# Diagonal blocks of 16 in place of 32 in the triangular inverse of a recurrence

## The chip, the core and the metric

The kernel runs on one core of one Trainium2 chip. The metric is the device time of one execution in microseconds (us), as the median of several executions. The engines are called as in the profile: PE is TensorE (matmul), PEld its weight loads, DVE is VectorE, ACT is ScalarE, POOL is GpSimd, and SP is SyncE, whose queue issues all of this kernel's transfers (DMA). Each engine works through its own instructions in order and waits for the others by semaphores.

## The reference

A two-layer decoder trunk on 1024 positions of width 1024, in float32. Layer 1 mixes by a recurrence (RWKV-7) over 16 heads of 64, layer 2 is differential attention over 8 heads, and a final norm ends it. The change lies in layer 1:

```
def step(state, inp):
    r_t, w_t, k_t, v_t, a_t, b_t = inp
    sa = einsum('bhij,bhj->bhi', state, a_t)
    state = (state * w_t[:, :, None, :] + sa[..., None] * b_t[:, :, None, :]
             + v_t[..., None] * k_t[:, :, None, :])
    y_t = einsum('bhij,bhj->bhi', state, r_t)
    return state, y_t
```

with `a = -kk` and `b = kk * a_h`, where `kk` is normalised per head. Around it stand four projections of 1024x1024 (r, k, v and the gate g), two small low-rank products (`w`, `a`), a group norm of `y`, the gate and an output projection.

## The kernel before

The recurrence is done in chunks of 64 positions. Within a chunk the steps that depend on each other are put into a lower triangular 64x64 matrix per head, and its inverse, `q`, turns the chunk's values into updates with plain matmuls. A pass works on 8 chunk-heads at once for each half of the partitions: two chunks (NC) times four head pairs (NU). There are 16 such passes ("chunk pairs"), each with five parts, written as generators:

- `prep` loads the pass's operands, forms the products of keys and decays on DVE and ACT, and multiplies them on PE into `pm` (the triangular matrix and its companions). The diagonal blocks go by way of `ab` to a DRAM buffer `dA` and come back transposed in meaning as `al`: one diagonal block per partition.
- `invert` inverts every diagonal block. DVE scales `al` by the reciprocals `ni` of its last row and sets the diagonal of `xx`. Then POOL substitutes forward, step by step: a product into `tm` (line 551) and a sum into `xx` (line 553), 31 times for blocks of 32. The result is stored to DRAM as `dX` and loaded as `qd`, which has the blocks' rows on the partitions.
- `merge` puts the two blocks of 32 of each chunk-head together to `q` (64x64): DVE transposes `qd`, PE multiplies with the off-diagonal block of `pm` (line 586), DVE and ACT copy the product out of PSUM (590, 591), PE multiplies again (597), and DVE and ACT copy it into `q` (600, 601).
- `chain` is the recurrence over the two chunks with the state on PE (lines 639, 649, 658 and the outputs 629, 632).
- `norm` does the group norm of the outputs (683, 693 on PE) and stores to `d_o`.

The slots run from -3 to 16. In slot i the code emits `chain` of pass i, `norm` of i-1, `merge` of i+1, `prep` of i+3 and `invert` of i+2, each spread over 13 ticks (T), and between them a budget of other work per slot (FILL): the projections that have not been done yet (lines 192 to 194 on PE, `fl`) and later a part of the output projection (lines 285 to 287). A planner then sets the order of all instructions: it simulates the program with durations of its own (Durations) and puts first what is ready and has the higher priority (PRI; chain over merge over invert over prep over the rest). So the order on each engine follows from the emitted code, but isn't written out in it.

What the steps touch: tiles `al` and `xx` have two buffers each; the PSUM tile `mg`, one buffer, is used by `merge` (two times a pass) and by `norm` (two times). The SP queue issues all transfers in one order, and the loads `al` (waits for `dA`) and `qd` (waits for `dX`) stand in it among the loads for the projections.

Of the kernel before, what the change touches and what calls it, by code (L numbers as in the profile page):

```python
# [20 lines left out]
P = 128  # L21
# [11 lines left out]
T = 13  # L33
# [43 lines left out]
class Trunk:  # L77
# [317 lines left out]
    def wkv_open(self):  # L395
        nc, tc = self.nc, self.tc
# [9 lines left out]
        cst = st.enter_context(tc.tile_pool(name="wcst", bufs=1, reuse_waits="tile"))  # L406
# [7 lines left out]
        for r0 in (0, 64):  # L414
            v = self.pmask[r0:r0 + 64].rearrange("p a (z t) -> p a z t", z=2)
# [8 lines left out]
        self.last = cst.tile([P, P], F32, name="last")  # L424
        nc.gpsimd.memset(self.last, 0.0)
        for o in (0, 64):
            nc.gpsimd.memset(self.last[o:o + 64, o + 31:o + 64:32], 1.0)
        self.omka = cst.tile([P, KT], F32, name="omka")
        nc.vector.tensor_scalar(self.omka, self.par[:, COL["a_k_a"], :], -1.0, 1.0, op0=ALU.mult, op1=ALU.add)
        self.state = [cst.tile([P, NU, C], F32, name=f"st{j}") for j in range(KT // NU)]  # L430
# [12 lines left out]
    def prep(self, M, following):  # L443

        nc, tp, ua, ps = self.nc, self.tp, self.ua[M["n"] // 2 % 2], self.sps
        j = M["j"]
        cc, kk, a, r, v = (M[n] for n in ("cc", "kk", "a", "r", "v"))
        M["dA"] = dA = self.dr.tile([8, 4, 32, 32], F32, name="dA")

        def ch(x):  # L450
            return x.rearrange("p u (c t) -> p (u c) t", t=C)
# [31 lines left out]
        ab = tp.tile([P, 8, 32], F32, name="ab")  # L483
# [24 lines left out]
        for b in range(4):  # L508
            bs = slice(32 * b, 32 * b + 32)
            nc.vector.tensor_tensor(ab[bs], ab[bs], pm[bs, b // 2, :, b % 2 * 32:b % 2 * 32 + 32], op=ALU.add)  # L510
        nc.sync.dma_start(out=dA.rearrange("c x s t -> (x s) c t"), in_=ab)
        yield 0
        M["bkt"] = bkt = ua.tile([P, 2, 8, C], F32, name="bkt")
        for h in range(2):
# [9 lines left out]
        nc.vector.tensor_tensor(v.rearrange("p u t -> p (u t)"), pp, v.rearrange("p u t -> p (u t)"), op=ALU.mult)  # L524
        M["bv"] = self.dr.tile([P, NU, TM], F32, name="d_bv", bufs=6)
        nc.sync.dma_start(out=M["bv"], in_=v)
        M["al"] = al = self.sb.tile([P, 32, 32], F32, name="al", bufs=2)
        nc.sync.dma_start(out=al, in_=dA.rearrange("c x s t -> (c x) (s t)").unsqueeze(0).to_broadcast([4, 32, 1024]))
        if following:
            self.load(following)  # L530

    def invert(self, M):

        nc, sb, sm = self.nc, self.sb, self.sm
        al = M["al"]
        yield 1
        ni = sm.tile([P, 32], F32, name="ni")
        nc.vector.tensor_scalar(ni, al[:, 31, :], 1e-24, -1.0, op0=ALU.max, op1=ALU.mult)
        nc.vector.reciprocal(ni, ni)
        nc.vector.tensor_tensor(al[:, 0:31], al[:, 0:31], ni.unsqueeze(1).to_broadcast([P, 31, 32]), op=ALU.mult)  # L540
        xx = sb.tile([P, 8, 32], F32, name="xx")
        nc.gpsimd.memset(xx, 0.0)
        for k in range(4):
            xq = xx[k * 32:k * 32 + 32].rearrange("p c t -> p (c t)")[:, k::36]
            nc.vector.tensor_copy(out=xq, in_=ni[k * 32:k * 32 + 32, k::4])  # L545
        yield 0
        for s in range(31):
            n, w = s // 4 + 1, 31 - s
            tm = sb.tile([P, 128], F32, name="tm", bufs=1)
            tv = tm[:, 0:n * w].rearrange("p (c t) -> p c t", t=w)  # L550
            nc.gpsimd.tensor_tensor(tv, al[:, s:s + 1, s + 1:].to_broadcast([P, n, w]),  # L551
                                    xx[:, 0:n, s:s + 1].to_broadcast([P, n, w]), op=ALU.mult)
            nc.gpsimd.tensor_tensor(xx[:, 0:n, s + 1:], xx[:, 0:n, s + 1:], tv, op=ALU.add)  # L553
            yield 0
        dX = self.dr.tile([32, 8, 4, 32], F32, name="dX")
        nc.sync.dma_start(out=dX.rearrange("x k q t -> q x k t"), in_=xx)
        M["qd"] = qd = self.ub.tile([P, 8, 32], F32, name="qd", bufs=1)
        nc.sync.dma_start(out=qd, in_=dX.rearrange("(c x) k q t -> (x k q) c t", c=8))

    def merge(self, M):  # L560

        nc, ps = self.nc, self.wps
        pm, ar, qd = M["pm"], M["ar"], M["qd"]
        M["q"] = q = self.ub.tile([P, 8, C], F32, name="q")

        M["uv"] = uv = self.ub.tile([P, 2, 8, C], F32, name="uv")
# [2 lines left out]
        for h in range(2):  # L569
            for c in range(NC):  # L570
                t0 = M["qt"] * TM + c * C
                src = self.d_vc[t0:t0 + C, e0:e0 + NU * P].rearrange("p (u z e) -> p u z e", z=2, e=64)[:, :, h, :]
                nc.sync.dma_start(out=uv[64 - h * 64:P - h * 64, h, c::NC, :], in_=src)
        yield 1
        x1 = self.ub.tile([P, 8, 32], F32, name="x1", bufs=1)
        nc.vector.transpose(x1, qd)
        for o in (0, 64):
# [152 lines left out]
    def layer1(self):  # L730
# [51 lines left out]
        for i in range(-3, 17):  # L782
            st_ = []
            if i == 13:
                fl = itertools.chain(fl, self.run(self.out_proj(512, 2, I["a_w_out"][0])))
            if 0 <= i < 16:
                st_.append((self.chain(Ms[i]), 8, 0, T))
            if 0 <= i - 1 < 16:
                st_.append((self.norm(Ms[i - 1]), 6, 0, T))
            if 0 <= i + 1 < 16:  # L790
                st_.append((self.merge(Ms[i + 1]), 9, 2, T))
            if 0 <= i + 3 < 16:
                st_.append((self.prep(Ms[i + 3], Ms[i + 4] if i < 12 else None), 12, 0, T))
            if 0 <= i + 2 < 16:
                st_.append((self.invert(Ms[i + 2]), 34, 0, T))
            self.slot(T, st_, fl, FILL[i + 3])
        for _ in fl:
            pass
# [539 lines left out]
```

## Time and profile before

| | us |
|---|---|
| median of 3 runs | 1633.68 |
| lowest, highest | 1631.85, 1635.23 |
| the profiled execution | 1635.44 |
| its span | 1633.6 |
| PE busy | 1494.4 |
| DVE busy | 1194.8 |
| ACT busy | 909.6 |
| POOL busy | 672.8 |

The profile is of one execution. Its span begins with its first instruction and ends with its last; the device time is 1.8 us longer. The profile's busy time of PE runs over pipelined matmuls with modelled ends, and PE's clock is granted at one of two levels, 1.2 or 2.4 GHz; the profile gives the granted clock of a stretch as a share of the full one. The kernel begins with norm, low-rank products and projections (to about 270 us), goes through the stage of the recurrence with the rest of the projections between it (to about 910 us), and then does layer 2.

### The profile page before, as it was taken

Reading aid. Unit: us, or ns where it says so; the run is one execution under the profiler, and the core shown is the slowest. Engines: PE = TensorE matmul, PEld = TensorE weight load, DVE = VectorE, ACT = ScalarE, POOL = GpSimd, SP = SyncE. Lnnn points to the kernel's source line nnn. Section 1 sums busy time; section 2 is a strip of 40 time slices with the busy share of each in tenths; the row PEclk is TensorE's granted clock in tenths of the full one; section 3 lists DMA queues with packets and bytes.
Section 4 is the critical chain, followed back from the end, with each engine's and each line's share of the span. In section 5 each row is a group of like instructions: output and inputs, shape, how many; then the busy total and the mean of one; then the engine's idle time right before and its main releaser. Section 6 shows DMA issues by size and latency. Waiting matters only on the chain.

```text
span 1633.6 us, 31095 instructions
## 1 busy us (share of the span) xinstructions
PE 1494.4 (91%) x10496; PEld 1208.3 (74%) x10496; DVE 1194.8 (73%) x3119; ACT 909.6 (56%) x2095; POOL 672.8 (41%) x1685
## 2 busy tenths in 40 slices
PE   3799999988998999979869789999999999999897
PEld 3577777666776777768758567788888888888786
DVE  7745658866879798788555777887878888787764
ACT  5645565745657586655234644665565656556420
POOL 4000003856878688778656111233232333333100
PEclk8799999989999999979879789999999999999999
DMA  7654677755656567656446451211111111113231
GB/s 195 187 185 144 186 226 216 201 163 152 194 157 175 164 179 190 185 160 174 128 142 164 131 169 58 67 46 31 46 46 27 46 33 40 40 40 119 92 126 52
DMA packets 218095, 207.39 MB, mean 127 GB/s; under 512 B 78032, under 2 KB 163280, under 8 KB 217936
## 3 DMA queue, kind: packets, MB, share of 16 engines
q1 hardware_dynamic: 217936, 205.40, 42.9%
q8 instruction: 83, 1.36, 0.3%
q14 instruction: 76, 0.62, 0.1%
HBM read 147.09 MB, written 58.27 MB: 126 GB/s over the span
## 4 chain that ended last, share of the span: by engine, by line
PE 63%; DVE 14%; DMA 7%; ACT 6%; issue 5%; POOL 4%; SPq 1%; ACTq 0%; DVEq 0%; POOLq 0%
PE pj L878 6%; PE pj L877 6%; PE pj L879 6%; PE fl L192 5%; PE fl L193 5%; PE fl L194 5%; PE tr L982 4%; PE sc L940 2%; PE sc L941 2%; PE tr L970 2%; POOL xx L553 2%; POOL tm L551 2%; DMA al<-dA 1%; PE sc L498 1%; PE tr L1255 1%
## 5 line engine op out<-in xcount | busy, mean ns | idle before, releaser
L192 PE MATMUL fl<-xh,wh 128*128 128x512 f32 x512 | 212.2, 420 | 11.2 <-DVE ev L217 8.8
L877 PE MATMUL pj<-wh,xh 128*128 128x512 f32 x512 | 214.1, 418 | 0.0
L193 PE MATMUL fl<-xl,wh 128*128 128x512 f32 x512 | 209.2, 410 | 3.7 <-DVE xl L151 3.7
L553 POOL TENSOR_TENSOR xx<-xx,tm 128x60 f32<-128x60 f32 (+24 forms) x496 | 196.8, 397 | 36.4 <-DVE xx L545 0.4
L194 PE MATMUL fl<-xh,wl 128*128 128x512 f32 x512 | 209.3, 410 | 0.0
L551 POOL TENSOR_TENSOR tm<-al,xx 128x60 f32<-128x60 f32 (+24 forms) x496 | 190.2, 383 | 40.4 <-DVE xx L545 4.0
L878 PE MATMUL pj<-wh,xl 128*128 128x512 f32 x512 | 202.7, 396 | 2.6 <-DVE xl L1216 2.6
L879 PE MATMUL pj<-wl,xh 128*128 128x512 f32 x512 | 202.1, 396 | 0.0
L157 DVE TENSOR_TENSOR wl<-wf,wh 128x512 fp32r<-128x512 f32 x160 | 119.0, 748 | 80.4 <-ACT wh L156 79.5
L946 ACT ACTIVATE p<-sc,mx 128x256 f32<-128x256 f32 (+7 forms) x128 | 94.6, 741 | 142.1 <-DVE mx L945 123.1
L926 POOL CAST kh<-kh 64x128 fp32r<-64x128 f32 x128 | 45.2, 353 | 263.4 <-ACT kh L918 250.0
L156 ACT CAST wh<-wf 128x512 fp32r<-128x512 f32 x160 | 97.6, 617 | 94.1 <-PE fl L193 71.6
L192 PEld LDWEIGHTS fl<-xh,wh 128*128 128x128 f32 x512 | 98.4, 192 | 40.3 <-issue 12.4
L193 PEld LDWEIGHTS fl<-xl,wh 128*128 128x128 f32 x512 | 99.0, 193 | 29.2 <-DVE xl L151 5.2
L194 PEld LDWEIGHTS fl<-xh,wl 128*128 128x128 f32 x512 | 98.7, 193 | 24.0 <-issue 1.4
L879 PEld LDWEIGHTS pj<-wl,xh 128*128 128x128 f32 x512 | 96.8, 189 | 21.9
L878 PEld LDWEIGHTS pj<-wh,xl 128*128 128x128 f32 x512 | 97.5, 190 | 19.6 <-DVE xl L1216 4.3
L877 PEld LDWEIGHTS pj<-wh,xh 128*128 128x128 f32 x512 | 97.5, 190 | 15.4 <-ACT xh L1215 0.2
L944 DVE TENSOR_REDUCE mx<-sc 128x1 f32<-128x256 f32 (+7 forms) x128 | 95.4, 753 | 0.8
L982 PEld LDWEIGHTS tr<-v,p 128*128 128x128 f32 x576 | 74.9, 194 | 7.8 <-ACT p L972 3.2
L982 PE MATMUL tr<-v,p 128*128 128x128 f32 x576 | 76.1, 278 | 2.1 <-ACT p L972 2.1
L940 PE MATMUL sc<-kh,q 128*128 128x512 f32 (+2 forms) x192 | 70.9, 378 | 4.0 <-issue 2.1
(295 smaller groups left out, 3695.3 us busy)
## 6 DMA issues: line engine op xcount, KB each, us to landing
wf<-in_a_w_in SPq DMA_DIRECT2D x64, 512.0 KB
d_in<-ev SPq DMA_DIRECT2D x64, 256.0 KB
wf<-in_b_w SPq DMA_DIRECT2D x64, 256.0 KB
xk<-d_xn SPq DMA_DIRECT2D x40, 256.5 KB
al<-dA SPq DMA_DIRECT2D x16, 512.0 KB
wf<-in_a_w_out SPq DMA_DIRECT2D x16, 512.0 KB
p<-d_x SPq DMA_DIRECT2D x10, 512.0 KB
d_c<-cc SPq DMA_DIRECT2D x16, 260.0 KB
```

The lines of the kernel that those rows point to most:

```text
L156: self.nc.scalar.copy(out=wh, in_=wf)
L157: self.nc.vector.tensor_tensor(wl, wf, wh.bitcast(F32), op=ALU.subtract)
L192: nc.tensor.matmul(G["ps"], lhsT=wh[:, kk, :], rhs=xh, start=(k == 0), stop=False)
L193: nc.tensor.matmul(G["ps"], lhsT=wh[:, kk, :], rhs=xl, start=False, stop=False)
L194: nc.tensor.matmul(G["ps"], lhsT=wl[:, kk, :], rhs=xh, start=False, stop=(k == KT - 1))
L551: nc.gpsimd.tensor_tensor(tv, al[:, s:s + 1, s + 1:].to_broadcast([P, n, w]), xx[:, 0:n, s:s + 1].to_broadcast([P, n, w]), op=ALU.mult)
L553: nc.gpsimd.tensor_tensor(xx[:, 0:n, s + 1:], xx[:, 0:n, s + 1:], tv, op=ALU.add)
L877: nc.tensor.matmul(pf, lhsT=self.X[i][0][:, k], rhs=wh, start=(k == 0), stop=False)
L878: nc.tensor.matmul(pf, lhsT=self.X[i][1][:, k], rhs=wh, start=False, stop=False)
L879: nc.tensor.matmul(pf, lhsT=self.X[i][0][:, k], rhs=wl, start=False, stop=(k == KT - 1))
L940: nc.tensor.matmul(sc[:, b:e], lhsT=q[:, m], rhs=H["kh"][:, m, b:e], start=True, stop=False)
L982: nc.tensor.matmul(po, lhsT=at[:, b, :], rhs=H["v"][:, b, :], start=(b == 0), stop=(b == i))
```

## The change

The diagonal blocks that POOL substitutes are 16x16 instead of 32x32. There are twice as many of them, in half as many steps, and 15 instead of 31 pairs of instructions.

In `prep`, two DVE instructions pick for every row the 16 columns of its own block out of `ab` (with a mask `hm` of two columns that says to which half of a block of 32 a row belongs) into `a2`. `dA`, `dX`, `al` and `xx` have half or a quarter of the size, and other leading dimensions. The load after the substitution is called `qc` (two buffers).

In `merge`, a further level comes first: ACT spreads `qc` into `qd` with the mask (block diagonal, 16 and 16), DVE transposes it (`x0`), PE multiplies with the blocks of `pm` on 32x32 tiles (32 matmuls of 16 columns), DVE scales the product out of PSUM into `g0`, PE multiplies with `qd` (32 matmuls again), and DVE adds the result to `qd`. From there the code is as before. All of it uses the `mg` buffer. `merge` now has 13 steps from tick 1 on instead of 9 from tick 2 on, and `invert` 18 instead of 34.

```diff
-            nc.gpsimd.memset(self.last[o:o + 64, o + 31:o + 64:32], 1.0)
+            nc.gpsimd.memset(self.last[o:o + 64, o + 15:o + 64:16], 1.0)
+        self.hm = cst.tile([P, 2], F32, name="hm")
...
+        self.g0 = cst.tile([P, 8, 32], F32, name="g0")
+        nc.gpsimd.memset(self.g0, 0.0)
...
-        M["dA"] = dA = self.dr.tile([8, 4, 32, 32], F32, name="dA")
+        M["dA"] = dA = self.dr.tile([8, 4, 2, 16, 16], F32, name="dA")
...
-        nc.sync.dma_start(out=dA.rearrange("c x s t -> (x s) c t"), in_=ab)
+        a2 = tp.tile([P, 8, 16], F32, name="a2")
+        nc.vector.tensor_scalar(a2, ab[:, :, 0:16], self.hm[:, 0:1], None, op0=ALU.mult)
+        nc.vector.scalar_tensor_tensor(a2, ab[:, :, 16:32], self.hm[:, 1:2], a2, op0=ALU.mult, op1=ALU.add)
+        nc.sync.dma_start(out=dA.rearrange("c x b s t -> (x b s) c t"), in_=a2)
...
-        M["al"] = al = self.sb.tile([P, 32, 32], F32, name="al", bufs=2)
-        nc.sync.dma_start(out=al, in_=dA.rearrange("c x s t -> (c x) (s t)").unsqueeze(0).to_broadcast([4, 32, 1024]))
+        M["al"] = al = self.sb.tile([P, 16, 16], F32, name="al", bufs=2)
+        nc.sync.dma_start(out=al, in_=dA.rearrange("c x b s t -> (c x b) (s t)").unsqueeze(0).to_broadcast([2, 64, 256]))
...
-        for s in range(31):
-            n, w = s // 4 + 1, 31 - s
+        for s in range(15):
+            n, w = s // 2 + 1, 15 - s
...
-        dX = self.dr.tile([32, 8, 4, 32], F32, name="dX")
+        dX = self.dr.tile([64, 8, 2, 16], F32, name="dX")
         nc.sync.dma_start(out=dX.rearrange("x k q t -> q x k t"), in_=xx)
-        M["qd"] = qd = self.ub.tile([P, 8, 32], F32, name="qd", bufs=1)
-        nc.sync.dma_start(out=qd, in_=dX.rearrange("(c x) k q t -> (x k q) c t", c=8))
+        M["qc"] = qc = self.ub.tile([P, 8, 16], F32, name="qc", bufs=2)
+        nc.sync.dma_start(out=qc, in_=dX.rearrange("(c x) k q t -> (x k q) c t", c=8))
...
         yield 1
+        qd = self.ub.tile([P, 8, 32], F32, name="qd", bufs=1)
+        for b in range(2):
+            nc.scalar.activation(qd[:, :, b * 16:b * 16 + 16], qc, AF.Copy, scale=self.hm[:, b:b + 1])
+        x0 = self.ub.tile([P, 8, 32], F32, name="x1", bufs=1)
+        nc.vector.transpose(x0, qd)
+        yield 1
+        pg = ps.tile([P, 8, 32], F32, name="mg", bufs=1)
+        for c in range(8):
+            for x in range(4):
+                r = slice(32 * x, 32 * x + 32)
+                nc.tensor.matmul(pg[r, c, 0:16], lhsT=pm[r, x // 2, c, x % 2 * 32:x % 2 * 32 + 32], rhs=x0[r, c, 0:16],
+                                 start=True, stop=True, tile_position=(32 * x, 32 * x))
+        yield 1
+
+        nc.vector.tensor_scalar(self.g0[:, :, 0:16], pg[:, :, 0:16], self.hm[:, 1:2], None, op0=ALU.mult)
+        yield 1
+        pq = ps.tile([P, 8, 32], F32, name="mg", bufs=1)
+        for c in range(8):
+            for x in range(4):
+                r = slice(32 * x, 32 * x + 32)
+                nc.tensor.matmul(pq[r, c, 0:16], lhsT=self.g0[r, c, :], rhs=qd[r, c, 16:32], start=True, stop=True, tile_position=(32 * x, 32 * x))
+        yield 1
+        nc.vector.tensor_tensor(qd[:, :, 16:32], qd[:, :, 16:32], pq[:, :, 0:16], op=ALU.add)
...
-                st_.append((self.merge(Ms[i + 1]), 9, 2, T))
+                st_.append((self.merge(Ms[i + 1]), 13, 1, T))
...
-                st_.append((self.invert(Ms[i + 2]), 34, 0, T))
+                st_.append((self.invert(Ms[i + 2]), 18, 0, T))
```

Since the planner orders anew, the change moves instructions that it doesn't name. Two places show it.

On the SP queue late in the stage, about where the profile stands at 812 us, the order of before has the load `al` and, as the next transfer, the store `dX` of another pass (shapes are those of the destination):

```order
L511 DMA dA<-ab 128x8x32
L292 DMA d_x_68<-ev 128x256
L700 DMA d_o<-yt 128x4x128
L679 DMA bv<-d_bv 128x512
L528 DMA al<-dA 128x1x1024
L556 DMA dX<-xx 4x256x32
L526 DMA d_bv<-v 128x512
L292 DMA d_x_68<-ev 128x256
L278 DMA ev<-in_x 128x256
```

In the changed kernel, around a `dX` (line 567) of the same part of the stage, the `al` before it stands some 18 rows earlier, and the load `qc` (line 569) follows with one transfer between:

```order
L584 DMA uv<-d_vc 64x4x64 x4
L292 DMA d_x_68<-ev 128x256
L734 DMA d_o<-yt 128x4x128
L713 DMA bv<-d_bv 128x512
L567 DMA dX<-xx 2x512x16
L278 DMA ev<-in_x 128x256
L569 DMA qc<-dX 128x8x16
L239 DMA wf<-in_a_w_out 128x4x256
L522 DMA dA<-a_9289 128x8x16
```

What moved is the distance between `al` and `dX`: in the order of before they stand side by side four times, in the new one never, and the nearest are four transfers apart.

On PE in the middle of the stage, the order of before has one group of the merge (line 586) between the recurrence's matmuls and the projections (`fl`):

```order
L658 MATMUL zu<-uv,bkt 64x64
L632 MATMUL y<-pm,uv 64x64
L194 MATMUL fl<-xh,wl 128x512
L192 MATMUL fl<-xh,wh 128x512
L658 MATMUL zu<-uv,bkt 64x64 x7
L632 MATMUL y<-pm,uv 64x64 x7
L586 MATMUL mg<-x_4463,pm 32x32 x16
L193 MATMUL fl<-xl,wh 128x512
L194 MATMUL fl<-xh,wl 128x512
```

The changed kernel has there the second of the new groups (line 606; 673, 663 and 683 are the recurrence's lines 639, 629 and 649), behind 19 matmuls of the projections that stand after the first:

```order
L194 MATMUL fl<-xh,wl 128x512
L673 MATMUL zu<-sv,pm 64x64 x8
L663 MATMUL y<-ar,sv 64x64 x8
L606 MATMUL mg<-qd,g_1999 32x16 x13
L683 MATMUL zu<-zs,q 64x64 x8
L606 MATMUL mg<-qd,g_1999 32x16 x19
L192 MATMUL fl<-xh,wh 128x512
L193 MATMUL fl<-xl,wh 128x512
```

What moved: the short matmuls of merge and recurrence stand together in longer rows, and the projections' matmuls between them are spread over the same number of passes.

## Rows read from the trace of the kernel before

**Rows 1.** The page: PE's busy time, and POOL's busy tenths in 40 slices.

```profile
PE 1494.4 (91%) x10496; PEld 1208.3 (74%) x10496; DVE 1194.8 (73%) x3119; ACT 909.6 (56%) x2095; POOL 672.8 (41%) x1685
...
POOL 4000003856878688778656111233232333333100
```

**Rows 2.** Five stretches: length, busy PE, PEld, DVE, ACT, POOL, then clock, DMA, GB/s.

```profile
314.00:438.00 124.00, 110.44 (x952) 83.36 (x951) 87.52 (x173) 69.25 (x143) 84.67 (x202) 0.88 0.60 169
438.00:666.00 228.00, 214.71 (x2150) 164.63 (x2149) 182.53 (x417) 154.73 (x308) 179.71 (x417) 0.97 0.64 180
666.00:743.00 77.00, 65.03 (x784) 53.09 (x783) 64.86 (x153) 42.21 (x90) 59.01 (x137) 0.87 0.63 168
743.00:829.00 86.00, 72.20 (x886) 64.59 (x886) 54.22 (x138) 35.99 (x75) 52.46 (x139) 0.92 0.51 143
829.00:910.00 81.00, 64.42 (x849) 56.25 (x851) 53.62 (x208) 40.50 (x85) 46.54 (x129) 0.84 0.52 147
```

**Rows 3.** Groups by line, 314 to 910 us: busy us, mean ns | idle before, releaser.

```profile
L553 POOL TENSOR_TENSOR xx<-xx,tm 128x60 f32<-128x60 f32 (+24 forms) x462 | 181.1, 392 | 33.5
L551 POOL TENSOR_TENSOR tm<-al,xx 128x54 f32<-128x54 f32 (+24 forms) x461 | 174.4, 378 | 33.8
...
L540 DVE TENSOR_TENSOR al<-al,ni 128x992 f32<-128x992 f32 x14 | 19.0, 1354 | 0.4
...
L597 PE MATMUL mg<-qd,x 32*32 32x32 f32 x512 | 11.9, 197 | 5.2 <-DVE yt L696 5.2
...
L576 DVE STREAM_TRANSPOSE x<-qd 128x256 f32<-128x256 f32 x16 | 6.9, 431 | 0.3 <-DMA qd<-dX 0.3
...
L600 DVE COPY q<-mg 32x256 f32<-32x256 f32 x16 | 6.5, 405 | 0.4 <-PE mg L597 0.3
```

**Rows 4.** POOL in order of time: start us, length us, instruction.

```profile
854.25 0.23 POOL L551 TENSOR_TENSOR tm<-al,xx 128x28 f32<-128x28 f32 x1
854.57 0.24 POOL L553 TENSOR_TENSOR xx<-xx,tm 128x28 f32<-128x28 f32 x1
...
884.00 0.87 POOL L553 TENSOR_TENSOR xx<-xx,tm 128x28 f32<-128x28 f32 x1
...
886.43 0.21 POOL L553 TENSOR_TENSOR xx<-xx,tm 128x8 f32<-128x8 f32 x1
```

**Rows 5.** The chain of work, matmul groups (two records per matmul): start, us, what.

```profile
329.12 0.99 PE mg L586 x32
...
433.84 0.62 PE mg L597 x32
...
817.84 0.98 PE mg L683 x8
```

**Rows 6.** The SP queue in order of time: start us, length of the issue, transfer.

```profile
588.77 0.57 SPq L556 DMA_DIRECT2D dX<-xx  x1
589.44 2.18 SPq L168 DMA_DIRECT2D wf<-in_a_w_in  x1
...
593.60 0.37 SPq L558 DMA_DIRECT2D qd<-dX  x1
...
743.40 3.92 SPq L526 DMA_DIRECT2D d_bv<-v  x1
...
775.49 0.57 SPq L528 DMA_DIRECT2D al<-dA  x1
776.11 0.55 SPq L556 DMA_DIRECT2D dX<-xx  x1
776.75 9.74 SPq L239 DMA_DIRECT2D wf<-in_a_w_out  x1
```

**Rows 7.** PE in order of time, three waits: in brackets idle us and releaser.

```profile
368.10 0.76 PE L192 MATMUL fl<-xh,wh 128*128 128x512 f32 x1 [5.10 <-DVE ev L217]
...
792.62 0.58 PE L285 MATMUL fl<-wh,xh 128*128 128x256 f32 x1 [7.09 <-DVE ev L291]
...
831.68 0.44 PE L639 MATMUL zu<-sv,pm 128*64 128x64 f32 x2 [8.92 <-DVE sv L665]
```

More of the change, by code (lines that the diff above doesn't have):

```diff
@@ L426, in wkv_open @@
         for o in (0, 64):
-            nc.gpsimd.memset(self.last[o:o + 64, o + 31:o + 64:32], 1.0)
+            nc.gpsimd.memset(self.last[o:o + 64, o + 15:o + 64:16], 1.0)
+        self.hm = cst.tile([P, 2], F32, name="hm")
+        for b in range(2):
+            v = self.ident.rearrange("p (x b j) -> p b x j", b=2, j=16)[:, b]
+            nc.vector.tensor_reduce(self.hm[:, b:b + 1], v, axis=AX.XY, op=ALU.add)
+        self.g0 = cst.tile([P, 8, 32], F32, name="g0")
+        nc.gpsimd.memset(self.g0, 0.0)
         self.omka = cst.tile([P, KT], F32, name="omka")
@@ L536, in invert @@
         yield 1
-        ni = sm.tile([P, 32], F32, name="ni")
-        nc.vector.tensor_scalar(ni, al[:, 31, :], 1e-24, -1.0, op0=ALU.max, op1=ALU.mult)
+        ni = sm.tile([P, 16], F32, name="ni")
+        nc.vector.tensor_scalar(ni, al[:, 15, :], 1e-24, -1.0, op0=ALU.max, op1=ALU.mult)
         nc.vector.reciprocal(ni, ni)
-        nc.vector.tensor_tensor(al[:, 0:31], al[:, 0:31], ni.unsqueeze(1).to_broadcast([P, 31, 32]), op=ALU.mult)
-        xx = sb.tile([P, 8, 32], F32, name="xx")
+        nc.vector.tensor_tensor(al[:, 0:15], al[:, 0:15], ni.unsqueeze(1).to_broadcast([P, 15, 16]), op=ALU.mult)
+        xx = sb.tile([P, 8, 16], F32, name="xx")
         nc.gpsimd.memset(xx, 0.0)
-        for k in range(4):
-            xq = xx[k * 32:k * 32 + 32].rearrange("p c t -> p (c t)")[:, k::36]
-            nc.vector.tensor_copy(out=xq, in_=ni[k * 32:k * 32 + 32, k::4])
+        for k in range(2):
+            xq = xx[k * 64:k * 64 + 64].rearrange("p c t -> p (c t)")[:, k::18]
+            nc.vector.tensor_copy(out=xq, in_=ni[k * 64:k * 64 + 64, k::2])
         yield 0
-        for s in range(31):
-            n, w = s // 4 + 1, 31 - s
-            tm = sb.tile([P, 128], F32, name="tm", bufs=1)
+        for s in range(15):
+            n, w = s // 2 + 1, 15 - s
+            tm = sb.tile([P, 64], F32, name="tm", bufs=1)
             tv = tm[:, 0:n * w].rearrange("p (c t) -> p c t", t=w)
@@ L554, in invert @@
             yield 0
-        dX = self.dr.tile([32, 8, 4, 32], F32, name="dX")
+        dX = self.dr.tile([64, 8, 2, 16], F32, name="dX")
         nc.sync.dma_start(out=dX.rearrange("x k q t -> q x k t"), in_=xx)
-        M["qd"] = qd = self.ub.tile([P, 8, 32], F32, name="qd", bufs=1)
-        nc.sync.dma_start(out=qd, in_=dX.rearrange("(c x) k q t -> (x k q) c t", c=8))
+        M["qc"] = qc = self.ub.tile([P, 8, 16], F32, name="qc", bufs=2)
+        nc.sync.dma_start(out=qc, in_=dX.rearrange("(c x) k q t -> (x k q) c t", c=8))
     def merge(self, M):
         nc, ps = self.nc, self.wps
-        pm, ar, qd = M["pm"], M["ar"], M["qd"]
+        pm, ar, qc = M["pm"], M["ar"], M["qc"]
         M["q"] = q = self.ub.tile([P, 8, C], F32, name="q")
@@ L574, in merge @@
         yield 1
+        qd = self.ub.tile([P, 8, 32], F32, name="qd", bufs=1)
+        for b in range(2):
+            nc.scalar.activation(qd[:, :, b * 16:b * 16 + 16], qc, AF.Copy, scale=self.hm[:, b:b + 1])
[18 more added lines that the diff above has]
+        nc.vector.tensor_tensor(qd[:, :, 16:32], qd[:, :, 16:32], pq[:, :, 0:16], op=ALU.add)
         x1 = self.ub.tile([P, 8, 32], F32, name="x1", bufs=1)
```

## Prediction, made before the changed kernel ran

> **What bounds the kernel now.** I read the page first: TensorE (PE) is busy for 91% of the span, GpSimd (POOL) for 41%, but POOL's work lies in slices 7 to 23 alone, where it is busy for six to eight tenths [rows 1]. This is the stage of the recurrence, about 300 to 910 us, and only there does the change do anything. Next I cut that stage into five stretches [rows 2]. The reader is to see two things in them. First, PE and POOL are both nearly full: in the quiet middle (438 to 666 us) PE is busy 214.7 of 228 us, and POOL 179.7 us; POOL pauses some 0.08 us after each of its 417 instructions (854.25 + 0.23 to 854.57, [rows 4]), another 33 us, so it is held for 213 of 228 us. Second, the other stretches lose more of PE: idle time plus the part taken by the clock (one minus the granted clock, times the length) is 13.3 + 6.8 us in the middle, 9%, but 13.6 + 14.9 of 124 us (23%) ahead of it, 12.0 + 10.0 of 77 (29%) and 13.8 + 6.9 of 86 (24%) behind it, and 16.6 + 13.0 of 81 (37%) in the last stretch. Together that is 121 us. So PE is the engine that ends the stage, its work is fixed, and the question is how much of those 121 us comes back against the work that is added to PE.
>
> Where the losses come from is read from the waits. Three of PE's longest end with VectorE (DVE) work, 5.10, 7.09 and 8.92 us [rows 7], but DVE was itself held: just ahead of each, the SP queue issued the load `al` and, as its next transfer, the store `dX`, and then took 9.74 us over an issue that otherwise takes a fraction of one; a `dX` that does not follow an `al` costs the next issue 2.18 us [rows 6]. The order of before has four such pairs (at 349, 389, 775 and 817 us; one stands in the rows), and all three waits follow one.
>
> **POOL and the DVE work around the substitution.** Before, a chunk pair has 31 steps of two instructions, 62, at a mean of 392 and 378 ns [rows 3]: 62 x 0.385 + 62 x 0.08 = 28.8 us. Now it has 15 steps, 30 instructions, of at most 36 elements per partition. Small ones take 0.23 us undisturbed and 0.87 us disturbed [rows 4]; I take 0.35, so 30 x 0.43 = 13 us. POOL gets some 16 us per slot back, 250 us in all. Taken by itself this buys little: none of PE's long waits [rows 7] ends with POOL. It matters through the tail and through POOL's full load, below. On DVE the product over `al` shrinks from 992 to 240 elements: 1.35 us [rows 3] becomes about 0.35. Four copies into `xx` become two. Against that stand two small instructions ahead of the store `dA`, one more transpose (0.43 us, the row of L576), a scaling and an addition that read PSUM (0.2 to 0.41 us each, the upper end from L600, [rows 3]): 1.4 us removed, 1.2 to 1.7 us added. I put DVE at zero; ScalarE gets two small instructions and is busy for two thirds of the middle stretch [rows 2], which hides them.
>
> **PE: the price.** Each merge gets two groups of 32 matmuls on 32x32 tiles, with 16 moving columns. The trace has groups of 16 of the same weight shape with 32 columns: 0.62 us at the full clock, 0.99 us at the lower [rows 5]. From below: half the columns at half the price, so a group of 32 costs 0.62 us. From above: the same price per matmul at the lower clock, 1.98 us. Which end is nearer is told by L683, where 2 moving columns still cost 0.98 us for eight records [rows 5]: narrow matmuls are paid by the weight load, not by columns. So I take the full-clock price per matmul, 1.24 us, 2.48 us per slot, 16 slots: **+39.7 us** (20 to 63). Nothing hides it, since PE is the engine that ends the stage.
>
> **PE: what comes back.** (a) In the new SP order no `dX` follows an `al` directly (4 transfers lie between at the least, 10 or more after the first slots), and `al` moves 128 KB instead of 512. The three waits are 21.1 us. The clock ahead of and behind the middle lies under its 0.97: 124 x 0.09 + 86 x 0.05 = 15.5 us [rows 2]. I take the waits and 10 of the clock, **-31 us** (0 to -37). (b) In the last stretch the two last substitutions share POOL, the later one ends at 886.6 us [rows 4], and the merge and the recurrence of that pair can only follow it. PE's loss there above the middle's rate of 9% is 29.6 - 7.3 = 22 us. With two substitutions shorter by 16 us each I take a little more than half, **-13 us** (0 to -22). (c) With POOL at half its load, the middle stretch, where POOL was held for 93%, loses less: its 20.1 us cannot all go; I take **-9 us** (0 to -14). (d) Against these: the tile `mg` has one PSUM buffer, which served two merge groups and two norm groups per slot and now serves six. PE waits 5.2 us in all for the norm's reader ahead of L597 [rows 3]; half as much again is **+3 us** (0 to 10).
>
> Behind the added steps of the merge PE has other work standing (mostly 5 to 20 matmuls of the projections, as the order shows), so the two extra trips to DVE and ScalarE cost nothing as long as that work is there; in the last slots, where it runs thin, they cost part of what (b) gives, which is why (b) is not taken whole. The wait on `dX` that holds SP ahead of the load of `qc`, and what stands behind it, is in the rivals.
>
> Sum: 39.7 - 31 - 13 - 9 + 3 = -10 us on the profiled run's 1635.4 us. That run lies 1.8 us above the median, so against the median 1633.7 - 10 = 1623 or 1624; I say **1624 us**.
>
> **A rule beside the rows.** What the trace shows: `dX`, 128 KB, has landed 4.83 us after its issue when the load `qd` that waits for it goes out [rows 6], with a leading dimension of 4 at its destination; the change makes that 2, with pieces of half the size and the same number of them. The Trainium skill, page "DMA: Bandwidth & Descriptors", section "Rules for kernel authors", says that an outermost dimension of few entries, such as a leading broadcast, confines a DMA to as many engines at most. By it `dX` and `al` would go from four engines to two; `dX` would have twice the pieces on each, while `al`, with a quarter of the bytes, would still have half on each. No row of before tells two engines from four. In the sum it changes nothing; it is behind the third rival.
>
> **Rivals.** 1. Slower: *the added matmuls are paid and the losses only change place*. In-order DVE and SP are re-planned, and other transfers meet instead; short matmuls in a row let the clock fall again. For it: the stretch 666 to 743 us lost 29% with no such pair in it [rows 2]. Price: +39.7 + 3 with a third of (a) to (c), -18: +25, so 1659. It decides where less than some 40 us of the 121 come back. 2. No change: the price of a group is as taken and 40 of the 53 come back: 1634. For it: the terms cancel nearly by themselves. 3. Slower: *the way back of the inverse*. If `dX` takes twice its 4.83 us, the load `qc` behind it holds SP 4.8 us longer in each of 16 slots, 77 us; half of it on the path is +39, so 1663. Against it: the inverse itself is done some 16 us earlier, and an SP issue of 3.92 us at 743 us [rows 6] has no PE wait of note behind it. It decides if PE's waits follow `dX`, slot by slot. 4. Faster by more: a group costs 0.62 us, as columns say: 20 us less, 1604. That the change doesn't do what it says is no case here: the order shows 480 POOL instructions in place of 992.
>
> **How the numbers follow.** The forecast, 1624, gets 0.37 and rival 4 0.16, so faster by over 0.2% (about 3.3 us, what a measurement of this kernel can tell from no change) is 0.53. Rival 2 gets 0.12. Rival 1 gets 0.27 and rival 3 0.08: slower 0.35. The range reaches from 14 us below rival 4, where nearly all of (a) to (c) comes back as well, to rival 1 and a little past it: 1590 to 1663. The forecast's own range, if it is faster, is 1600 to 1630.
>
> **What will show it.** The two new groups in the trace: 1.24 us each (1.1 to 1.4) or nearer 0.62. POOL's two substitution lines: 480 instructions, about 170 us busy, not 387. The SP queue: no issue of 8 us or more behind `al` and `dX`. The granted clock between 314 and 438 us: near 0.97. The stage's last stretch: PE's loss under 25%. The time from `dX` to `qc`: 4.8 us or nearer 9.7. I am wrong if PE's idle time plus clock loss in the stage stays at 110 us or more, or if the groups cost 2 us each.

## The result: 1.1 % slower, and what the profile after shows

| | before | changed |
|---|---|---|
| median, us (4 runs each) | 1634.45 | 1653.66 |
| lowest, highest | 1631.85, 1639.30 | 1649.16, 1658.58 |
| ratio, 95% interval | | 1.0107 [1.0075, 1.0138] |
| profiled execution, its span | 1635.44, 1633.6 | 1658.58, 1656.9 |

The forecast was 1624, faster. It came out slower by 19 us, inside the range (1590 to 1663), near the first rival's 1659 and the third's 1663. The profiled run of the changed kernel is the slowest of its four, so the two spans below differ by 23 us.

The page of the changed kernel, against [rows 1]: GpSimd is relieved as planned, 434.8 us in place of 672.8, and TensorE is busier by 34 us.

```profile
PE 1528.1 (92%) x12544; PEld 1238.1 (75%) x12544; DVE 1185.4 (72%) x3169; ACT 922.0 (56%) x2127; POOL 434.8 (26%) x1174
...
POOL 4010013443323324233320011233333333333100
...
L562 POOL TENSOR_TENSOR tm<-al,xx 128x30 f32<-128x30 f32 (+10 forms) x240 | 74.5, 310 | 59.7 <-DVE xx L556 39.4
...
L564 POOL TENSOR_TENSOR xx<-xx,tm 128x30 f32<-128x30 f32 (+10 forms) x240 | 73.2, 305 | 18.1
```

To see where the stage lost its time, both kernels have to be cut at the same places of the program, since equal times are not equal work. The cuts here are the issues on the SP queue of the 1st, 7th, 11th and 16th store `d_o`, one per pass. The end is the start of what follows the stage, 648.5 us before the end of the span in both. Columns as in [rows 2]: length, busy PE, PEld, DVE, ACT, POOL, clock, DMA, GB/s. First the kernel before, cut that way:

```profile
280.00:436.41 156.41, 142.85 (x1112) 107.72 (x1111) 113.65 (x219) 92.10 (x187) 113.87 (x259) 0.90 0.60 171
436.41:658.25 221.84, 208.55 (x2084) 159.66 (x2083) 178.60 (x409) 148.74 (x297) 174.97 (x405) 0.97 0.65 181
658.25:813.98 155.73, 136.19 (x1647) 116.23 (x1645) 119.17 (x283) 80.98 (x170) 115.08 (x282) 0.90 0.58 159
813.98:953.46 139.48, 111.77 (x1194) 95.19 (x1191) 88.72 (x317) 65.78 (x140) 54.94 (x158) 0.83 0.50 146
953.46:985.10 31.64, 26.93 (x115) 20.80 (x114) 24.89 (x79) 15.99 (x43) 3.94 (x12) 0.89 0.58 182
280.00:985.10 705.10, 626.29 (x6141) 499.60 (x6140) 525.02 (x1304) 403.59 (x837) 462.79 (x1114) 0.91 0.59 167
```

And the changed kernel:

```profile
280.00:424.53 144.53, 133.97 (x1411) 101.26 (x1410) 103.01 (x214) 85.54 (x180) 62.53 (x158) 0.89 0.54 148
424.53:676.77 252.24, 241.07 (x3001) 185.72 (x3001) 186.34 (x446) 163.85 (x327) 83.57 (x221) 0.97 0.57 162
676.77:825.64 148.87, 129.15 (x1939) 109.45 (x1940) 103.31 (x274) 77.40 (x165) 49.75 (x141) 0.81 0.48 130
825.64:951.41 125.77, 109.27 (x1641) 96.00 (x1635) 84.26 (x291) 61.77 (x133) 18.72 (x50) 0.84 0.54 157
951.41:1008.40 56.99, 47.90 (x199) 38.11 (x199) 36.91 (x126) 25.51 (x65) 10.64 (x32) 0.85 0.41 128
280.00:1008.40 728.40, 661.37 (x8177) 530.54 (x8177) 513.83 (x1348) 414.07 (x867) 225.22 (x601) 0.89 0.53 149
```

Read the last row of each: TensorE idles 78.8 us before and 67.0 after, but the clock takes 63.5 us (0.09 of 705) before and 80.1 (0.11 of 728) after. The losses together are 142 and 147 us. So the whole loss did not shrink but grew by 5 us, and the added work came on top: busy time less the clock's part is 562.8 us before and 581.2 after, 18 us more. The worst stretch is the third, where the clock falls from 0.90 to 0.81. The fourth, the thinning end of the recurrence, is better as forecast: 51 us of loss became 37. But the fifth, behind the last store, lost 17.6 us where it had lost 8.2, so over the two of them 5 us are left. (It also had more to do, 47.9 us busy for 26.9: work moves between the stretches even with these cuts.)

How one of the waits there comes about can be read from three queues of the changed kernel. SP first:

```profile
714.50 0.53 SPq L567 DMA_DIRECT2D dX<-xx  x1
715.14 5.16 SPq L256 DMA_DIRECT2D xm<-d_o  x2
720.39 0.38 SPq L522 DMA_DIRECT2D dA<-a  x1
722.05 0.37 SPq L569 DMA_DIRECT2D qc<-dX  x1
```

then DVE, with idle time and releaser in brackets:

```profile
718.20 0.69 DVE L488 TENSOR_TENSOR bk<-kraw,a 64x512 f32<-64x512 f32 x1
722.74 0.69 DVE L259 TENSOR_TENSOR xm<-xm,xk 128x512 f32<-128x512 f32 x1 [3.85 <-DMA xm<-d_o]
723.47 0.41 DVE L634 COPY q<-mg 32x256 f32<-32x256 f32 x1
```

and PE:

```profile
717.68 2.08 PE L533 MATMUL sc<-sq,bones 128*128 128x512 f32 x2
724.03 0.45 PE L683 MATMUL zu<-zs,q 64*64 64x64 f32 x2 [4.27 <-DVE q L634]
```

The store `dX` is issued at 714.50; the two loads `xm` behind it hold the queue for 5.16 us; DVE, which works in order, stands 3.85 us before the product that needs `xm`; the copy of `q` is behind that product, and TensorE stands 4.27 us for `q`. It is the same pattern as `al` and `dX` in [rows 6] and the waits of [rows 7], without an `al` next to it. In the whole stage the issues right behind `dX` took 55.9 us in the 16 slots of before (their own length of some 0.4 us each included), of which 35.4 behind the four pairs, and 67.9 us in the changed kernel, with no pair at all: none longer than 5.41 us, but a long one in nearly every slot. From `dX` to `qc` it is now 7.5 to 9.9 us, where `qd` came 4.8 to 6.1 us behind a `dX` that stood alone (11.3 to 12.4 in the pairs).

A third thing hangs on `dX`: GpSimd. Its memset of the next `xx` (line 542 before, 553 after) waits for the store to be done with that tile. Over the stage (waited for: us, times, longest), before:

```profile
POOL xx L542 <- DMA dX<-xx: 47.9, 10, 13.0
```

and in the changed kernel:

```profile
POOL xx L553 <- DMA dX<-xx: 93.4, 14, 9.4
```

So part of the time that GpSimd got back went into a longer wait for the store.

The added groups on PE, at the full clock:

```profile
309.39 0.72 PE L596 MATMUL mg<-x,pm 32*32 32x16 f32 x64
310.05 0.50 PE L192 MATMUL fl<-xh,wh 128*128 128x512 f32 x1
```

310.05 - 309.39 = 0.66 us for 64 records, 10 ns each, where the 32 records of L597 with 32 columns took 0.62 us [rows 5], 19 ns each. Half the columns cost half; the two groups of 16 passes come to 2 x 0.66 x 16 = 21 us, not 39.7. (Their busy time in the stage is 12.9 and 16.3 us, since some ran at the lower clock.)

### The profile page after: what moved, and what is told of

Same layout as the page of the kernel before. It is cut to its first block, busy times and chain, and to the rows that moved or that the text cites. A ratio compares the mean times of both kernels' runs of the same rounds, so it can differ in the third digit from the quotient of the medians.

```text
span 1656.9 us, 34761 instructions
## 1 busy us (share of the span) xinstructions
PE 1528.1 (92%) x12544; PEld 1238.1 (75%) x12544; DVE 1185.4 (72%) x3169; ACT 922.0 (56%) x2127; POOL 434.8 (26%) x1174
## 4 chain that ended last, share of the span: by engine, by line
PE 64%; DVE 12%; DMA 10%; ACT 6%; issue 4%; POOL 2%; SPq 1%; DVEq 0%; ACTq 0%; POOLq 0%
PE pj L911 6%; PE pj L912 6%; PE pj L913 6%; PE fl L192 5%; PE fl L193 5%; PE fl L194 5%; PE tr L1016 4%; PE sc L974 2%; PE sc L975 2%; PE tr L1004 2%; DMA xm<-d_o 2%; PE sc L505 1%; DMA dX<-xx 1%; PE zu L673 1%; PE tr L1288 1%
## 5 line engine op out<-in xcount | busy, mean ns | idle before, releaser
L157 DVE TENSOR_TENSOR wl<-wf,wh 128x512 fp32r<-128x512 f32 x160 | 115.1, 724 | 77.6 <-ACT wh L156 74.6
L156 ACT CAST wh<-wf 128x512 fp32r<-128x512 f32 x160 | 97.2, 616 | 92.5 <-PE fl L193 83.7
L978 DVE TENSOR_REDUCE mx<-sc 128x1 f32<-128x256 f32 (+7 forms) x128 | 95.7, 754 | 0.8
L562 POOL TENSOR_TENSOR tm<-al,xx 128x30 f32<-128x30 f32 (+10 forms) x240 | 74.5, 310 | 59.7 <-DVE xx L556 39.4
L1016 PEld LDWEIGHTS tr<-v,p 128*128 128x128 f32 x576 | 74.5, 193 | 11.3 <-ACT p L1006 6.7
L564 POOL TENSOR_TENSOR xx<-xx,tm 128x30 f32<-128x30 f32 (+10 forms) x240 | 73.2, 305 | 18.1
```

The lines of the kernel that those rows point to most:

```text
L156: self.nc.scalar.copy(out=wh, in_=wf)
L157: self.nc.vector.tensor_tensor(wl, wf, wh.bitcast(F32), op=ALU.subtract)
L978: nc.vector.tensor_reduce(c, sc[:, 0:n], axis=AX.X, op=ALU.max)
L1016: nc.tensor.matmul(po, lhsT=at[:, b, :], rhs=H["v"][:, b, :], start=(b == 0), stop=(b == i))
```

## Experiments

Ratios are to the kernel before, run on the same chip. "Loss" is TensorE's idle time and what the clock took, worked out as above from the row from 280 us to 648.5 us before the end of the span (taken as the same in all versions); it is of one profiled run each, and the clock's part is an upper bound, as not all work scales with the clock.

**Relief, short matmuls, transfers.** Four kernels. The kernel before with every second step of the substitution left out (its inverse is incomplete), so GpSimd's relief without anything else:

```diff
-        for s in range(31):
+        for s in range(0, 31, 2):
...
-                st_.append((self.invert(Ms[i + 2]), 34, 0, T))
+                st_.append((self.invert(Ms[i + 2]), 18, 0, T))
```

> The kernel before, with every second step of the substitution left out (16 of 31 steps, 512 POOL instructions instead of 992, spread over 18 ticks' steps as in the changed kernel); blocks of 32, transfers and merge as before. The inverse is not computed rightly, the work is otherwise the same. It measures POOL's relief alone. Theory L (PE's work sets the stage; its losses only change place): within 6 us of before, 1628 to 1640. Theory W (the relief is real, but the slower way back of the inverse, dX on a leading dimension of 2, takes it): 1610 to 1620.

1640.57 us, 0.9988 [0.9963, 1.0014]. The relief alone is worth nothing here, although GpSimd's time in the span falls to 484.8 us: the loss is 142 us as before, and GpSimd's wait for `dX` is 64.5 us in place of 47.9.

The changed kernel with each new group of 32 short matmuls replaced by one wide one (the values are not those wanted):

```diff
-        for c in range(8):
-            for x in range(4):
...
+        nc.tensor.matmul(pg[:, :, 0:16], lhsT=pm[:, 0, 0, :], rhs=x0[:, :, 0:16], start=True, stop=True)
```

> The changed kernel with each of the two new groups of 32 short matmuls replaced by one matmul of 128 rows and 128 columns into the same PSUM tile (wrong values, same waits, same DVE and ScalarE steps). It takes 16 x (1.32 - 0.54) = 12.5 us of PE work away, the two groups having taken 0.66 us each and a single matmul of that size some 0.27. Theory L: 12 us faster than the changed kernel, about 1641. Theory W: no more than 5 us faster, 1648 to 1654. A third view, that rows of short matmuls lower the granted clock, gives more than 12 us: 1635 or less, with the clock of the stage back at 0.91.

1627.83 us, 0.9923 [0.9902, 0.9944]: by the ratios 1.8 %, 30 us, below the changed kernel, for 13 to 17 us of work left out (a group takes 0.66 us, the wide matmul 0.14 to 0.25). How much of that is the work and how much a new order can only be told with several orders of each kernel, below.

The changed kernel with `al` as two loads and `dX` as two stores of 64 partitions, so that no transfer has a leading dimension of 2:

```diff
-        nc.sync.dma_start(out=al, in_=dA.rearrange("c x b s t -> (c x b) (s t)").unsqueeze(0).to_broadcast([2, 64, 256]))
+        for k in range(2):
+            nc.sync.dma_start(out=al[k * 64:k * 64 + 64], in_=dA.rearrange("c x b s t -> (c x b) s t"))
...
-        nc.sync.dma_start(out=dX.rearrange("x k q t -> q x k t"), in_=xx)
+        for k in range(2):
+            nc.sync.dma_start(out=dX[:, :, k, :], in_=xx[k * 64:k * 64 + 64])
```

> The changed kernel with the store dX written as two stores of 64 partitions and the load al as two loads of 64 partitions, so that no leading dimension is 2; same bytes, same pieces, two more transfers per slot. By the Trainium skill's rule on leading dimensions dX should land in well under the 7.6 us from its issue to the load qc (3 to 4 us), and SP should not be held for 4 to 5 us behind it. Theory W: 12 to 20 us faster than the changed kernel, 1634 to 1642. Theory L: the waits go, but PE's time does not, within 6 us of it, 1648 to 1658.

1593.95 us, 0.9716 [0.9685, 0.9746]: by the ratios 3.9 %, 64 us, below the changed kernel and faster than before by 2.8 %. Far more than either theory had. The SP queue of this kernel at about the same time (one pass further on), and the stage as a whole:

```profile
712.50 1.22 SPq L569 DMA_DIRECT2D dX<-xx  x2
713.80 0.57 SPq L292 DMA_DIRECT2D d_x<-ev  x1
714.97 0.93 SPq L239 DMA_DIRECT2D wf<-in_a_w_out  x1
717.03 0.37 SPq L571 DMA_DIRECT2D qc<-dX  x1
```

```profile
280.00:937.40 657.40, 623.40 (x8182) 500.93 (x8181) 515.72 (x1349) 412.94 (x868) 223.89 (x604) 0.96 0.59 166
```

The issue behind `dX` is no longer held (0.57 us; in the same pass of the changed kernel, at 755 us, it took 5.41), `qc` follows the first of the two stores after 4.5 us (8.2 there), and the loss of the stage is 34.0 + 26.3 = 60 us in place of 147.

The same for the kernel before, with four loads and four stores of 32 partitions:

> The kernel before with dX written as four stores of 32 partitions and al loaded by four loads of 32 partitions, so that no leading dimension is 4. It tests the prediction's step (a): if the pairs of al and dX on the SP queue cost before 21 us of PE waits and 10 of clock, this is 15 to 30 us faster, 1605 to 1620. If losses only change place (theory L): within 8 us of before, 1626 to 1642.

1611.49 us, 0.9828 [0.9796, 0.9860]. The kernel before gains from it as well.

**Which transfer, and the order by itself.** The changed kernel with only `dX` split, then only `al`; both split and the groups replaced as in the second kernel above (so again without the values wanted); and a control, in which only a constant of the planner is moved (the time in ns that it assumes for a transfer), so that the same instructions come in another order:

```diff
-LATER, BACK, MOVING, SLOWER, SCAN = 1000, 4000, 1.3, 105, 550
+LATER, BACK, MOVING, SLOWER, SCAN = 1100, 4000, 1.3, 105, 550
```

> The changed kernel, with the store dX alone as two stores of 64 partitions; al stays one load with a leading dimension of 2. Theory X (the store dX is what holds the SP queue: 7.5 to 9.9 us from dX to qc in every slot, against 2.8 to 7.2 us with both split): 0.970 to 0.985 of the kernel before, most of the 60 us that both together gave. Theory A (the load al is what costs): no nearer than 1.000, as the changed kernel. Theory O (the new order that the planner makes of any edit is what gave the 60 us, not the transfers): nothing systematic, anywhere between 0.97 and 1.01.

> The changed kernel, with the load al alone as two loads of 64 partitions; dX stays one store with a leading dimension of 2. Theory X: 1.000 to 1.011 of the kernel before, and dX to qc still 7.5 us or more in every slot. Theory A: 0.970 to 0.985. Theory O: anywhere between 0.97 and 1.01.

> Both transfers split, and each of the two new groups of 32 short matmuls replaced by one matmul of 128 columns, so that the merge of the two halves of a block is left out in effect (the value is not what the reference wants). It prices the groups once the transfers are fast: 2 x 0.66 us less about 2 x 0.1 us, in 16 slots, is 18 us of work. If TensorE's work sets the stage then: 0.960 to 0.963 of the kernel before, against 0.972 with the groups. If short matmuls also lower the clock: 0.955 or less. If the groups hide in waits: 0.968 or more.

> The changed kernel, same instructions and same transfers, but one constant of the planner moved (1000 to 1100), so that the order is planned afresh. It prices the order by itself. Theories X and A: within 8 us of the changed kernel, 1.006 to 1.016 of the kernel before. Theory O: 10 us or more away from it, on either side; then no gain of a split may be put down to the transfer alone without a look at the trace.

`dX` alone: 1606.03 us, 0.9810 [0.9779, 0.9841]. `al` alone: 1618.20, 0.9888 [0.9862, 0.9914], where 1.000 or more had been expected if `dX` alone counts. Both and no short matmuls: 1570.78, 0.9597 [0.9572, 0.9622]. The control: 1633.31 us, **0.9988 [0.9966, 1.0010]**, 20 us below the changed kernel with not one instruction changed. That is the size of the whole result. In the control the stretch from the 7th to the 9th `d_o`, its first row here, loses 6.0 us of idle time and 12.0 by the clock, 18; in the changed kernel, below it, 14.8 and 24.0, 39.

```profile
664.24:730.83 66.59, 60.63 (x893) 49.75 (x891) 55.11 (x138) 41.32 (x88) 21.52 (x59) 0.82 0.56 154
```

```profile
676.77:754.04 77.27, 62.47 (x879) 51.70 (x880) 54.81 (x139) 42.60 (x89) 24.16 (x71) 0.69 0.50 138
```

**Several orders of each kernel.** The same edit with other values (1010, 1100 and later 1030 for the kernel before; 1030 and 990 for the changed one).

> The kernel before, same instructions and transfers, one constant of the planner moved by a hundredth (1000 to 1010), so that the order is another. Theory N (any one order is a draw of some 20 us; the order of before is a usual one): 0.99 to 1.01 of the kernel before. Theory T (the order of before was a lucky one, so that the change was measured against it and lost for that): 1.008 to 1.02.

> The kernel before with the same constant at 1100: a third order of the same instructions. Theory N: 0.99 to 1.01 of the kernel before. Theory T: 1.008 to 1.02.

> The kernel before with the planner's constant at 1030: a fourth order of its instructions, so that four orders of each kernel stand against each other. If before's own order is a usual one: 0.993 to 1.003 of the kernel before. If it is the best of its orders, as the two others (1.010 and 1.006) say: 1.004 to 1.012.

> The changed kernel with the constant at 1030: a third order of its instructions, next to 1.011 (as changed) and 0.999 (at 1100) of the kernel before. If the change as such costs nothing or little and the order of the changed kernel was an unlucky one: 0.99 to 1.002. If the changed kernel is slower by its added work in most orders: 1.005 to 1.015.

> The changed kernel with the constant at 990: a fourth order. If the order of the changed kernel was an unlucky one: 0.99 to 1.002 of the kernel before. If the changed kernel is slower in most orders: 1.005 to 1.015.

| kernel | constant | ratio, 95% | idle + clock loss, us | held behind `dX`, us |
|---|---|---|---|---|
| before | 1000 | 1 | 78.8 + 63.5 | 55.9 |
| | 1010 | 1.0104 [1.0068, 1.0140] | 84.0 + 87.3 | 69.2 |
| | 1100 | 1.0064 [1.0041, 1.0086] | 83.7 + 79.5 | 71.5 |
| | 1030 | 1.0181 [1.0140, 1.0223] | 95.7 + 88.3 | 60.0 |
| changed | 1000 | 1.0107 [1.0075, 1.0138] | 67.0 + 80.1 | 67.9 |
| | 1100 | 0.9988 [0.9966, 1.0010] | 50.7 + 70.5 | 55.6 |
| | 1030 | 1.0020 [0.9994, 1.0047] | 55.6 + 72.4 | 67.8 |
| | 990 | 0.9975 [0.9939, 1.0011] | 62.1 + 64.5 | 68.1 |

The order in which the kernel before was measured is the fastest of its four, that of the changed kernel the slowest of its four. The means are 1.0087 and 1.0023: the change is faster by 0.65 %, 10.5 us, in the mean over orders. With a standard deviation of 0.0076 and 0.0059 between orders, that difference is known to about 1.2 % (95%), so its sign isn't settled. Nothing here says whether 1000 is a chance value for the kernel before or had been chosen because it was fast. The losses agree in direction: 165 us in the mean before (142, 171, 163, 184), 131 after (147, 121, 128, 127), against 21 us of added work. How long SP is held behind `dX` doesn't sort the orders.

**Do the transfers hold in other orders, and the dose.** Both split transfers in another order (constant 1030 for the changed kernel, 1010 for before); the split kernel before with half the substitution left out; and the changed kernel with the suspected cost doubled:

```diff
+        dY = self.dr.tile([64, 8, 2, 16], F32, name="dY")
+        nc.sync.dma_start(out=dY.rearrange("x k q t -> q x k t"), in_=xx)
         nc.sync.dma_start(out=dX.rearrange("x k q t -> q x k t"), in_=xx)
```

> The changed kernel with both transfers split, in another order (the planner's constant 1030 in place of 1000). Theory S (the split is worth some 40 to 50 us in whatever order): 0.965 to 0.982 of the kernel before. Theory O (the 0.972 of the first order was a lucky draw): above 0.985, at the level of the unsplit orders (0.998 to 1.011).

> The kernel before with both transfers split, in another order (the planner's constant 1010 in place of 1000; without the split that order gave 1.010). Theory S: 0.975 to 0.992. Theory O: 0.998 or more.

> The kernel before with both transfers split and every second step of the substitution left out (the inverse is not the right one): GpSimd's relief alone, with fast transfers. If the relief was worth nothing (0.999 without the split) because slow transfers took it: 0.960 to 0.972, against 0.983 with the split alone. If GpSimd doesn't set the stage at all: 0.978 to 0.992, an order's draw around the split alone.

> The changed kernel with the store dX doubled: the same store with a leading dimension of 2 goes first to a scratch tensor that nobody reads, then to dX. It doubles the suspected cost. Theory S (slow stores hold the SP queue, and so TensorE): dX's pair holds it some 4 to 8 us more per slot, and the kernel is 20 us or more above the mean of its orders, 1.015 to 1.04 of the kernel before. If the store's slowness is hidden and only the order counts: 0.998 to 1.011.

> The changed kernel with both transfers split, and the planner told that what it reads back from dX and dA lands 2 us sooner than it had assumed (4000 to 2000), since it does now. If the planner's wrong guess still costs something: below 0.968 of the kernel before. If it is one more order: 0.966 to 0.976.

The last one is the split changed kernel with the planner's assumed delay of what is read back cut from 4000 to 2000: 1596.12 us, 0.9755 [0.9708, 0.9802], one more order and no gain. The others:

| kernel | ratio, 95% | loss, us |
|---|---|---|
| before, split (first order) | 0.9828 [0.9796, 0.9860] | 110 |
| before, split, other order | 0.9780 [0.9758, 0.9801] | 109 |
| before, split, half the substitution | 0.9605 [0.9569, 0.9641] | 68 |
| changed, split (first order) | 0.9716 [0.9685, 0.9746] | 60 |
| changed, split, other order | 0.9707 [0.9675, 0.9738] | 68 |
| changed, split, no short matmuls | 0.9597 [0.9572, 0.9622] | 56 |
| changed, `dX` stored twice | 1.0478 [1.0454, 1.0502] | 219 |

The doubled store, in the SP queue of that kernel:

```profile
724.04 0.53 SPq L568 DMA_DIRECT2D dY<-xx  x1
724.62 4.78 SPq L569 DMA_DIRECT2D dX<-xx  x1
729.82 5.56 SPq L736 DMA_DIRECT2D d_o<-yt  x1
...
737.61 0.36 SPq L571 DMA_DIRECT2D qc<-dX  x1
```

The second store is itself held 4.78 us, the issue behind it 5.56, and `qc` goes out 13.0 us after `dX`. It costs 75 us against the mean of the changed orders, 4.7 us per slot for some 5.5 us more from `dX` to `qc` (8.1 to 13.6 in the mean of 16). It is more than the 1.015 to 1.04 that had been expected. This is far outside what orders do, and so are the splits of `dX`: all split versions lie below every unsplit one, though `al` alone, 0.9888, only 0.9 % below the fastest order of the changed kernel. Whether the held queue, the late `qc` or GpSimd's wait for the store is what costs isn't told apart, since every edit of `dX` moved all three. GpSimd's wait is 36.0 us with `dX` split and 185.5 with it doubled:

```profile
POOL xx L553 <- DMA dX<-xx: 36.0, 11, 5.4
POOL xx L553 <- DMA dX<-xx: 185.5, 14, 18.0
```

With `al` alone split the three hardly moved (65 us behind `dX`, `qc` after 7.6 to 10.1 us, GpSimd 89.1 us), and in the changed kernel the issue right behind `al` took 0.3 to 0.7 us and DVE waited for `al` 1.1 us in all. So none of these explains what splitting `al` gained, 1.35 % against the mean of the orders; that stays open.

## Why the prediction was wrong, step by step

**Where the 19 us are from.** In the measured pair the step that failed is what was to come back. Steps (a) to (c) took 53 us off the losses, above all (a); the losses rose by 5 us, and 18 us of work came on top. Why they did so in this pair is in part the order. In the mean over orders the change gives -10.5 us, the forecast's -10 within an uncertainty that is larger than the number. That agreement is luck: the added work was 21 us and not 43, and the losses fell by 34 us and not by 53, so two errors cancel. The measured pair is off that mean by two draws: the changed kernel's order lies 0.84 % (14 us) above the mean of its four, before's 0.87 % (14 us) below its own. The sum compared two orders as if they were one; it had no term for re-planning, where the same instructions in another order came out up to 1.8 % apart, and no range for it. Rival 1 said that "the losses only change place", which describes the pair (142 and 147 us), but it was argued with short matmuls and other meetings of transfers, not with the draw. What in this order lets the clock fall in the third stretch, beyond waits such as the one shown, wasn't settled.

**The price of the groups** was mis-sized: 21 us, not 39.7. The step that failed took L683's price per record for a rule on narrow matmuls; L683 has another weight shape, 128x128 where the groups have 32x32. Rival 4 had the right price, 0.62 for 0.66, and not the result. With split transfers, leaving the groups out gives 0.9597 against a mean of 0.9726 for the three split orders: 21 us, one order against three and so uncertain by some 17, for 13 to 17 us of work. A cost of the short matmuls beyond their columns, the second half of rival 1's reason (they lower the clock), isn't seen in that, nor ruled out.

**Step (a), -31 us,** failed in its reason. It is true that the pairs of `al` and `dX` went, and the holds of 7.6 to 9.7 us with them. But the step left a `dX` that stands alone as it was, 2.18 us [rows 6], which would be 35 us over 16 slots, and it was this very store that the edit changed: 67.9 us were held. The first and third stretch lost 29 + 35 = 64 us before and 26 + 48 = 74 after. The rule that had been weighed and put down as one that "changes nothing" in the sum was the one to price. What the rows show: `dX` is 1024 pieces in both kernels, and takes 4.8 us with a leading dimension of 4 and 7.5 with 2, at best. If the pieces are shared by as many engines as that dimension has entries, 256 and 512 per engine, that is 10.5 ns a piece on top of 2.1 us, and 16 engines with 64 pieces each would take 2.8 us, an estimate: the split version's shortest time is 2.8 (its second store goes out some 0.6 us behind the first, so the agreement is rough). No view here shows the engines of a transfer. That sharing, up to 16 engines, is what the Trainium skill says (page "DMA: Bandwidth & Descriptors", section "Rules for kernel authors"); the three times agree with it. The same section of the Trainium skill advises against two transfers to disjoint halves of the partitions, since both would use all engines anyway. Here `dX` in halves gained 35 us (0.9810 against the mean 1.0023) and both transfers 49 (0.9726), which fits an undivided transfer that does not use them all; the measurement decides.

**Rival 3, the way back of the inverse,** had the mechanism (7.5 to 9.9 us from `dX` to `qc`, in all 16 slots; 4.7 us of time per slot when doubled), and was given too little, 0.08. But it does not explain the difference of the two kernels: splitting the transfers gives 46 us in the kernel before (1.0087 to 0.9804, means) and 49 in the changed one. Before lost as much in its few long holds and on `al` as the changed kernel in its many short ones.

**Steps (b) and (c), the relief of GpSimd,** were priced at 22 us together. (b) came out in the fourth stretch alone, whose loss fell by 14.8 us where 13 were said; with the fifth, 5 us are left. (c) did not: 20 us lost in the second stretch before, 19 in a longer one after. By itself the relief is worth nothing (0.9988; 1 % if the mean of before's orders is the measure, which is within their spread). With the transfers split it is worth 0.9804 to 0.9605, 2 %, 33 us, in the one order that was run. So the relief showed only once the transfers were split; that GpSimd's 93 % in the middle was a bound behind the slow store is argued from this. Split against split, the change brings 33 - 21 = 12 us by these parts, and 0.9804 to 0.9726, 13 us, as a whole (known to about 0.8 %, so its sign isn't settled either).

**Step (d), +3 us,** was small and of the wrong sign: TensorE's waits ahead of groups in `mg` are 13.3 us in all before and 5.6 in the changed kernel.

**The POOL line** was right: 480 instructions and 147.7 us, where about 170 were said. Rival 2's sum left out the 3 us of (d): 39.7 + 3 - 40 gives 1636, not 1634. Two signs failed: the clock between 314 and 438 us was 0.86, not near 0.97, and the fourth and fifth stretch lost 29 and 31 %, not under 25. Of the two conditions named for being wrong, one held: the losses of the stage stayed above 110 us.

The best version measured that does all the work is the changed kernel with both transfers split, 0.9716 and 0.9707 in two orders, 2.8 to 2.9 % faster than before.

## What to carry to other kernels

Where a planner draws the order anew for every edit, a single build of each version compares two draws: here equal instructions gave up to 1.8 % between orders, more than the edit was worth. Build a few orders of both, or look for effects that are larger. When an edit changes a transfer's shape, price the transfer from its new outermost dimension and count pieces per engine, and ask what is queued behind it. And a resource that is full, like GpSimd here, need not be the one that pays when it is relieved: here the worth of relief showed only after the transfers were fast.

## What the runs showed of the hardware

- In groups of matmuls on 32x32 tiles at four positions, the cost went by the columns down to 16 of them: 10 ns a record with 16, 19 ns with 32.
- Behind a `dX` with a leading dimension of 2 at its destination, the next issue on the SP queue took up to 5.41 us in the changed kernel; with two such stores in a row, the second took 4.78 us and the issue behind it 5.56. Cut in two along the partitions, the same bytes left the next single issue at 0.3 to 1.0 us.
- Over the stage the clock was 0.96 in the split version, with 34 us of idle time of TensorE, and 0.88 with the doubled store, with 124. Between such extremes it did not go by idle time alone: 0.91 before with 78.8 us, 0.89 in the changed kernel with 67.0.
